# Linear attention on one Trainium2 core: when the first octet's output is stored

## The chip, the core and the metric

The kernel runs on one core of one Trainium2 chip. The metric is the device time of one execution in microseconds (us), as the median of several runs. The engines are named as in the profile: PE (TensorE; PEld is its weight load), DVE (VectorE), ACT (ScalarE), POOL (GpSimd, which here only issues the loads) and SP (SyncE, which issues the stores).

## The reference

Linear attention with a ReLU feature map, for 8 batches, 12 heads, 512 positions and 64 features, all in f32:

```python
Q_feat = np.maximum(0, Q)
K_feat = np.maximum(0, K)
KV = np.einsum('bhkd,bhkv->bhdv', K_feat, V)
K_sum = np.sum(K_feat, axis=2)
numerator = np.einsum('bhqd,bhdv->bhqv', Q_feat, KV)
denominator = np.einsum('bhqd,bhd->bhq', Q_feat, K_sum)
return (numerator / (denominator[:, :, :, None] + 1e-10)).astype(np.float32)
```

## The kernel before

The 96 heads (batch times head) are taken in 12 *octets* of eight. K and V are loaded in 24 groups of four heads, two groups to an octet, as tiles of 128 partitions by 16 rows of 64 features; Q in one tile of 128 by 32 rows for each octet. The loads turn f32 into bf16 on the way (all but the first K and V group, which SP loads as f32). Each K or V load writes 256 KB and reads 512 KB, each Q load writes 512 KB and reads 1 MB. One octet's output is 1 MB of f32.

**Loads.** All loads but the first two are issued by POOL, in the order of the code: for each octet K, V, K, V, Q (`load_k` L93, `load_v` L97, `load_q` L101). There are 12 buffers each for K and V tiles and 7 for Q tiles.

**The work of one octet.** `prep` (L139, L141) and `prep_v` (L146 on ACT, L148 on DVE) apply the ReLU to K and spread K and V over head-wise masked copies; `mm_kv` (L153) multiplies them on PE and `evac_kv` (L163) copies the result to SBUF. `qt` transposes Q on PE (`transp`, L174) and ACT applies the ReLU (`relu_q`, L182). `denom` (L224 on PE, L227, L232 and L236 on DVE) makes the reciprocals of the denominators. `out_t` (L204 on PE, L206 on ACT) makes the transposed numerators. `backs` transposes them back in two halves (`back`, L242), normalises each half on DVE (`norm`, L248) and calls `store`. The order of the work is written out by hand: in the loop over octets, the transposes back, the normalisation and the store of octet o - 1 stand behind the K-V products of octet o; in the last octets this is shifted (`SAME`). The last octet is written out by itself and its store goes in two halves (L261).

**Stores.** `store` issues on SP. `DELAY` is 5, and there are 7 output buffers of 1 MB; the f32 tile of the first K and V group uses one of them at the start. Ahead of an octet's store, SP issues a tiny DMA (L256) of 64 bf16 numbers from the K tile of group 2(o + 5) to a scratch tile nobody reads. It can only be issued when that K load has landed, and since SP issues in order, the store (L263) behind it waits for the load too. The first seven octets, 0 to 6, have such a K tile (groups 10, 12, ... 22); from octet 7 on, the store waits only for its own normalisation. Each tiny DMA also writes the scratch tile that the one before wrote, so it waits for that one to land.

Of the kernel before, what the change touches and what calls it, by code (L numbers as in the profile page):

```python
# [10 lines left out]
def kernel(  # L11
# [20 lines left out]
    NO = NG // 2  # L32
    assert NO * 8 == NH and R == 16 and RQ == 32
    DELAY = 5
# [217 lines left out]


    def store(o, o_sb):
        if o + DELAY < NO:
            nc.sync.dma_start(out=scratch, in_=k_sb[2 * (o + DELAY)][0:1, 0, :])  # L256
        Ov = Or[o].rearrange("p (r d) -> p r d", d=D)
        if o == NO - 1:
            for j in range(2):
                rs = slice(RQ // 2 * j, RQ // 2 * (j + 1))  # L260
                nc.sync.dma_start(out=Ov[:, rs], in_=o_sb[:, rs])  # L261
            return
        nc.sync.dma_start(out=Ov, in_=o_sb)  # L263
# [22 lines left out]
    def backs(o):  # L286
        o_sb = out_tile()
        for j in range(2):
            norm(o, j, back(o, j), o_sb)
        store(o, o_sb)  # L290
# [26 lines left out]
    o = NO - 2  # L317
# [15 lines left out]
    for i in range(2):  # L333
        relu_q(o + 1, i, transp(o + 1, i), nc.vector if i == 1 else None)
    norm(o, 1, ps, o_sb)
    store(o, o_sb)
    idle(5, o + 1)
    out_u(o + 1, 0)
# [32 lines left out]
```

## Time and profile before

| what | value |
|---|---|
| median of 3 runs | 126.78 us (126.53 to 127.32) |
| the profiled execution: its time | 127.21 us |
| the profiled execution: its span, first to last instruction | 125.4 us |
| busy: PE, DVE, ACT, POOL | 69%, 64%, 63%, 26% of the span |
| loads issued by POOL: share of the 16 DMA engines | 77.1% |
| stores, tiny DMAs and first loads issued by SP: share of the 16 DMA engines | 27.0% |
| traffic at the DRAM over the span | 401 GB/s |
| first octet's normalisation (L248) | 23.20 to 25.56 us |
| first tiny DMA and first store issued | 42.14 and 42.77 us |
| last store's first half issued | 118.76 us |

All times within the execution are counted from the span's start. Lines such as L248 are lines of the kernel printed above. In a row of a timeline the first two numbers are the start and the duration, then come the engine (SPq is SP's queue of DMA issues), the line, the operation, out<-in, and in brackets how long the engine sat idle before it and what ended that. In the view by windows the columns are the stretch and its length, busy time and number of instructions on PE, PEld, DVE, ACT and POOL, the granted PE clock as a share of full speed, the DMA share and the GB/s moved, as bytes written. In the rows of DMA queues, q0 holds POOL's loads and q1 what SP issues: packets, megabytes and share of the 16 engines.

### The profile page before, as it was taken

The page shows a single profiled execution, that of the slowest core. Times are in us where ns is not written, and L with a number is a line of the kernel's source. Part 1 is how long each engine was busy: PE and PEld are TensorE (multiplying, and loading weights), DVE is VectorE, ACT ScalarE, POOL GpSimd, SP SyncE. Part 2 cuts the span into 40 slices and gives each one's busy share as a digit, 9 for nine tenths or more (in the row PEclk, how much of TensorE's full clock was granted, in tenths as well). Part 3 has the DMA queues.
Part 4 walks back from the last instruction along what each step waited for, and adds up shares of the span by engine and source line. Part 5 has one row for each costly group of instructions (what it writes and reads, how often), then busy time and mean ns, then how long its engine had stood idle before and what let it go on. Part 6 is the DMA issues. An engine that isn't in the chain of part 4 may idle for free.

```text
span 125.4 us, 2673 instructions
## 1 busy us (share of the span) xinstructions
PE 86.5 (69%) x1075; PEld 78.7 (63%) x1075; DVE 80.3 (64%) x176; ACT 79.5 (63%) x114; POOL 32.9 (26%) x64
## 2 busy tenths in 40 slices
PE   0056779979598992891698596199867767797700
PEld 0055669879397881880697494199766566696600
DVE  2686175697968979289047839632946937989620
ACT  0383895898979977686329787364929828637300
POOL 6953324333162431241133115034031000000000
PEclk9999986999999999998559999657999999999997
DMA  4999999999999999999999999999999999999992
GB/s 148 299 218 201 214 206 211 213 211 215 206 214 206 210 189 323 246 218 310 269 215 282 301 212 262 323 208 240 339 220 216 334 247 214 325 427 421 426 412 103
DMA packets 10748, 32.15 MB, mean 256 GB/s; under 512 B 1392, under 2 KB 1392, under 8 KB 9328
## 3 DMA queue, kind: packets, MB, share of 16 engines
q0 software_dynamic: 8352, 18.35, 77.1%
q1 hardware_dynamic: 2384, 13.63, 27.0%
q8 instruction: 8, 0.13, 0.4%
q14 instruction: 4, 0.03, 0.1%
HBM read 37.75 MB, written 12.58 MB: 401 GB/s over the span
## 4 chain that ended last, share of the span: by engine, by line
DMA 61%; DVE 15%; PE 14%; issue 2%; POOL 1%; DVEq 1%; ACT 0%; POOLq 0%
DMA v_sb<-in_V_dram 37%; DMA q_sb<-in_Q_dram 24%; DVE o_sb L248 8%; PE ps_kv L153 6%; PE ps_bk L242 4%; PE ps_qt L174 3%; DVE kf L139 2%; DVE vo L141 1%; POOL k_sb L93 1%; DVE vo L148 1%; DVEq L366 1%; DVE den L232 1%; DVE rec L236 1%; DVE qt L180 1%; DVE own L227 1%
## 5 line engine op out<-in xcount | busy, mean ns | idle before, releaser
L153 PE MATMUL ps_kv<-vo,kf 128*128 128x132 bf16 x384 | 31.3, 248 | 13.3 <-ACT vo L146 7.8
L248 DVE TENSOR_TENSOR o_sb<-ps_bk,rec 128x1024 f32<-128x1024 f32 x24 | 28.3, 1219 | 16.9 <-PE ps_bk L242 16.9
L153 PEld LDWEIGHTS <-kf 128*128 128x128 bf16 x384 | 29.1, 112 | 14.3 <-DVE vo L141 6.9
L163 ACT CAST kvd<-ps_kv 64x260 bf16<-64x260 f32 (+1 forms) x54 | 18.7, 346 | 19.4 <-PE ps_kv L153 18.2
L182 ACT ACTIVATE qt<-ps_qt 128x1024 bf16<-128x1024 bf16 x23 | 22.4, 1022 | 9.2 <-PE ps_qt L174 9.1
L139 DVE TENSOR_SCALAR kf<-k_sb,mask 128x1024 bf16<-128x1024 bf16 x46 | 19.2, 459 | 10.0 <-DMA k_sb<-in_K_dram 10.0
L206 ACT COPY ot_sb<-ps_ot 128x1024 f32<-128x1024 f32 x22 | 21.9, 1014 | 2.4 <-PE ps_ot L204 1.6
L174 PE MATMUL ps_qt<-ident,q_sb 128*128 128x128 bf16 x192 | 16.0, 250 | 10.6 <-DMA q_sb<-in_Q_dram 10.6
L242 PE MATMUL ps_bk<-ident,ot_sb 128*128 128x128 f32 x192 | 23.0, 273 | 0.0
L93 POOL DMA_DIRECT2D k_sb<-in_K_dram x23 | 12.7, 554 | 35.0 <-DMA q_sb<-in_Q_dram 22.3
L174 PEld LDWEIGHTS <-q_sb 128*128 128x128 bf16 x192 | 13.9, 114 | 12.5 <-DMA q_sb<-in_Q_dram 12.5
L242 PEld LDWEIGHTS ps_bk<-ident,ot_sb 128*128 128x128 f32 x192 | 20.9, 141 | 0.0
L97 POOL DMA_DIRECT2D v_sb<-in_V_dram x23 | 13.1, 570 | 19.8 <-DMA k_sb<-in_K_dram 10.5
L204 PE MATMUL ps_ot<-qt,kvd 128*128 128x256 bf16 x88 | 12.7, 271 | 4.5 <-DVE o_sb L248 4.5
L141 DVE TENSOR_SCALAR vo<-v_sb,mask 128x1024 bf16<-128x1024 bf16 x23 | 11.2, 485 | 3.1 <-DMA v_sb<-in_V_dram 3.1
L146 ACT ACTIVATE vo<-v_sb,mask 128x1024 bf16<-128x1024 bf16 x11 | 12.7, 1152 | 0.3
L204 PEld LDWEIGHTS <-kvd 128*128 128x128 bf16 x88 | 8.2, 97 | 6.7 <-issue 6.0
L224 PEld LDWEIGHTS <-qt 128*128 128x128 bf16 x192 | 6.7, 96 | 4.7 <-ACT qt L182 3.4
L224 PE MATMUL ps_den<-kvd,qt 128*128 128x16 bf16 x192 | 7.5, 179 | 2.7 <-ACT qt L182 2.1
L101 POOL DMA_DIRECT2D q_sb<-in_Q_dram x12 | 6.5, 541 | 7.3 <-DMA v_sb<-in_V_dram 5.8
L227 DVE SCALAR_TENSOR_TENSOR own<-ps_den,mask_h 128x256 f32<-128x256 f32 x12 | 5.0, 416 | 3.1 <-PE ps_den L224 3.1
L148 DVE TENSOR_SCALAR vo<-v_sb,mask 128x1024 bf16<-128x1024 bf16 x12 | 5.8, 480 | 0.0
(27 smaller groups left out, 26.2 us busy)
## 6 DMA issues: line engine op xcount, KB each, us to landing
out_dram<-o_sb SPq DMA_DIRECT2D x11, 1024.0 KB, 9.1
q_sb<-in_Q_dram POOLq DMA_DIRECT2D x12, 512.0 KB, 14.8
k_sb<-in_K_dram POOLq DMA_DIRECT2D x23, 256.0 KB, 13.7
v_sb<-in_V_dram POOLq DMA_DIRECT2D x23, 256.0 KB, 13.2
out_dram<-o_sb SPq DMA_DIRECT2D x2, 512.0 KB, 4.4
kv_first<-in_K_dram SPq DMA_DIRECT2D x1, 512.0 KB, 3.2
kv_first<-in_V_dram SPq DMA_DIRECT2D x1, 512.0 KB, 4.0
scratch<-k_sb SPq DMA_DIRECT2D x7, 0.1 KB, 4.8
```

Of the source, the lines that this page charges most:

```text
L93: nc.gpsimd.dma_start(out=k_sb[g].rearrange("p r d -> p (r d)"), in_=Kr[g], single_packet=True)
L97: nc.gpsimd.dma_start(out=v_sb[g].rearrange("p r d -> p (r d)"), in_=Vr[g], single_packet=True)
L139: nc.vector.tensor_scalar(kf[g][:, :, s, :], k_sb[g], scalar1=0.0, scalar2=mask[:, 0, s:s + 1], op0=Alu.max, op1=Alu.mult)
L153: nc.tensor.matmul(ps_kv[:, g % 2, 0:2 * (D + 2)].rearrange("p (t d) -> p t d", t=2), kf[g][:, r, :, :].rearrange("p s d -> p (s d)"), vo[ ...
L163: copy(kvd[o % NK][64 * c:64 * c + 64, 4 * gs.start + s:4 * gs.stop:2, c * D1:c * D1 + D1].rearrange("p (g t) d -> p g t d", t=2), ps_kv[6 ...
L174: nc.tensor.transpose(ps[:, u, :], q_sb[o][:, i * (U // 2) + u, :], ident)
L182: nc.scalar.activation(to, ps, Act.Relu)
L204: nc.tensor.matmul(ps[:, i], kvd[o % NK][:, h, 1:2 * D + 1], q[:, :, h, :], start=True, stop=True, skip_group_check=True)
L206: nc.scalar.copy(ot[o][:, :, 4 * j:4 * j + 4], ps.rearrange("p h u c -> p u h c"))
L224: nc.tensor.matmul(ps[:, u], qt_sb[o % NZ][:, u, :], kvd[o % NK][:, :, 0:2 * D1:2 * D1 - 1], start=True, stop=True, skip_group_check=True)
L242: nc.tensor.transpose(ps[:, 2 * v:2 * v + 2].rearrange("p c d -> p (c d)"), ot[o][:, 8 * j + v].rearrange("p h c -> p (h c)"), ident32)
L248: nc.vector.tensor_tensor(o_sb[:, rs], ps, rec[o][:, rs].unsqueeze(2).to_broadcast([P, 16, D]), op=Alu.mult)
```

## The change

The condition ahead of the tiny DMA gets a lower bound. Octet 0's store is then issued without a tiny DMA ahead of it, when octet 0 has been normalised. Octets 1 to 6 keep theirs, with the same K groups (12 to 22); octets 7 to 11 had none and have none. No other line differs.

```diff
     def store(o, o_sb):
-        if o + DELAY < NO:
+        if 0 < o < NO - DELAY:
             nc.sync.dma_start(out=scratch, in_=k_sb[2 * (o + DELAY)][0:1, 0, :])
         Ov = Or[o].rearrange("p (r d) -> p r d", d=D)
```

## The prediction

> **What bounds the kernel now.** I read the page's slices first, then the timelines of SP, POOL, PE and DVE, the chain of waits, and windows of time at the end. The slices of DMA share and of moved bytes come first:
>
> ```profile
> DMA  4999999999999999999999999999999999999992
> GB/s 148 299 218 201 214 206 211 213 211 215 206 214 206 210 189 323 246 218 310 269 215 282 301 212 262 323 208 240 339 220 216 334 247 214 325 427 421 426 412 103
> HBM read 37.75 MB, written 12.58 MB: 401 GB/s over the span
> ```
>
> The reader is to see that the transfers never rest. Up to slice 14 the rate is about 211 GB/s, but loads turn f32 in DRAM into bf16 on chip, so 211 written means 422 read. At the end, where only stores run, it is 421 to 427. Both kinds therefore run at the same traffic of some 420 GB/s at the DRAM. 50.33 MB between 2.0 and 123.2 us is 415 GB/s, so the whole kernel is within 2% of those two rates.
>
> Next, the SP queue, which issues the stores, in order of time:
>
> ```profile
> 42.14 0.59 SPq L256 DMA_DIRECT2D scratch<-k_sb  x1
> 42.77 0.57 SPq L263 DMA_DIRECT2D out_dram<-o_sb  x1
> 52.63 0.51 SPq L256 DMA_DIRECT2D scratch<-k_sb  x1
> 53.19 0.58 SPq L263 DMA_DIRECT2D out_dram<-o_sb  x1
> ...
> 103.38 0.50 SPq L256 DMA_DIRECT2D scratch<-k_sb  x1
> 103.97 11.65 SPq L263 DMA_DIRECT2D out_dram<-o_sb  x5
> 118.76 1.46 SPq L261 DMA_DIRECT2D out_dram<-o_sb  x2
> ```
>
> Each tiny copy waits until its K load has landed and the store follows at once. So these starts are also landing times: K load 10 at 42.14, 12 at 52.63, 22 at 103.38. From 12 to 22 that is five octets in 50.75 us, 10.15 each, with one store in each. Without a store, the transposes' waits put Q's tile 2 at about 26.2 (POOL's release at 26.18) and tile 4 at 40.92: 7.37 us an octet. One store of 1.05 MB thus costs the loads 2.5 us (bytes over 420 GB/s) to 2.8 us (10.15 less 7.37).
>
> The chain of waits then says who follows whom late in the kernel:
>
> ```profile
> 64.80 16.10 DMA q_sb<-in_Q_dram
> 80.89 0.05 issue
> 80.94 1.89 PE ps_qt L174 x16
> ...
> 118.74 1.13 DVEq L366
> ```
>
> Up to 80.89 the chain is loads; behind Q's tile 8 it is PE and DVE work only, 38 us of it. And the transfers at the end, by windows of two microseconds:
>
> ```profile
> 118.00:120.00 2.00, 0.34 (x4) 0.11 (x1) 1.87 (x2) 0.00 (x0) 0.00 (x0) 1.00 1.02 432
> 120.00:122.00 2.00, 0.00 (x0) 0.00 (x0) 0.00 (x0) 0.00 (x0) 0.00 (x0) 1.00 0.98 406
> ```
>
> The last two columns are DMA share and GB/s. The transfers are still full while the last store is issued, so the end is bound by bytes and by the last octet's work together.
>
> **The change part by part.** Everything is compared with this execution: span 125.4, its time 127.21, so 1.81 lies around the span; the median of the runs, 126.78, is 0.43 under that time.
>
> Removed: one tiny copy (0.59 us of SP's issue, 0.1 KB) and the wait ahead of it. The wait was 40.5 us, but nothing but stores is queued on SP and no octet waits for a store (buffer 0 of the outputs comes round again at octet 7, whose normalisation is at about 87). It also drops the wait of the second copy for the first one to land (4.7 us, over at 47.7, five before 52.63). Worth: 0, hidden under the wait for K load 12; without that cover 0.6 us.
>
> Moved: the first store, one DMA of 1 MB with 0.57 us of issue. It goes from 42.77 to the end of the first octet's normalisation:
>
> ```profile
> 23.20 2.36 DVE L248 TENSOR_TENSOR o_sb<-ps_bk,rec 128x1024 f32<-128x1024 f32 x2 [2.40 <-PE ps_bk L242]
> ```
>
> so 23.20 + 2.36 = 25.56. SP is idle there; on SP it passes no other transfer. On the engines it passes the loads on POOL's queue that are outstanding then and up to 42: the rest of octet 3's, octet 4's, and octet 5's first. How soon is it served? For store 0 as it was, issued at 42.77, the SP queue's packets in a window tell it:
>
> ```profile
> q0 software_dynamic: 225, 0.43, 113.5%
> ...
> q1 hardware_dynamic: 62, 0.42, 51.6%
> q0 software_dynamic: 52, 0.15, 43.9%
> ```
>
> The first line is 42.8 to 44.8, where q1 has no line at all; the others are 46.8 to 48.8, where the store takes half of the engines' time. So a store is served 4 us late and then over some 5 us. Moved, it is served from about 30 to 35.
>
> Cost there: loads that land after about 31 are 2.5 to 2.8 us later, I take 2.5. Q's tile 3 moves from 34.1 to about 36.5, tile 4 from 40.9 to 43.4, K load 10 from 42.1 to 44.6. Gain later: between K loads 10 and 12 there is no store now, so that stretch is 7.4 to 8 us, not 10.49, and K load 12 lands at 44.6 + 7.5 = 52.1 against 52.63. The two cancel, since the same bytes lie ahead of K load 12 in both orders. I bound the remainder: 10.49 is 0.34 over the later mean of 10.15, which could be a cost of starting the mixture and might be saved or moved; so -0.5 to +0.3, and I take -0.1.
>
> What does the lateness do to the compute? One octet takes PE 6.88 us when loads are there (first transpose of octet 5 at 50.49 to the last output product at 57.37). Octet 2's work on PE ends at 33.3 and now waits to 36.5 rather than 34.13. From 36.5 it needs till 43.4, where tile 4 arrives; then till 50.3, and tile 5 arrives at 50.5 to 51. Before, PE sat 2.39 us idle ahead of tile 5: that idle time is the cover and pays for the delay. From octet 6 on the waits for Q tiles (3.19 at 60.56, 1.09 at 70.87, 2.56 at 80.94) and all transfers are as they were.
>
> One thing on PE can go worse. The wait ahead of tile 3 grows to about 3.2 us, and in this execution a wait of 3.19 us ahead of octet 6 went with a granted clock of 0.50 from 60 to 64; that octet took 60.56 to 69.78, 9.22 us, 2.34 more than octet 5. Paid in octet 3, PE would be at 45.7, 52.6 and 59.5 at the ends of octets 3, 4 and 5, still ahead of tile 6 at 60.56: worth 0 by these rows. The Trainium skill, in "TensorE: Matmul & The Clock Gate", Part 1, says that the half rate follows an idle window of about 3.4 us that runs freely, so that a wait's place in the window decides; the trace agrees in its stretches of 6.8 us at 0.5 from 58.9 and 79.4, and by it the loss in octet 3 is a matter of luck from run to run, 0 or 2.34 there.
>
> Sum: 0 (copy) + 2.5 (loads late early) - 2.6 (no store between K loads 10 and 12) + 0 (compute, covered) = -0.1 us. 127.21 - 0.1 = 127.1 for a like execution, and 126.78 - 0.1 = 126.7 for the median.
>
> **The rivals.**
>
> A, the early stage swallows the store (faster): if the loads before 42 have room to spare, the 2.5 us there cost nothing and the 2.5 us after K load 10 are won to the end: 126.78 - 2.5 = 124.3. For it: compute has tiles in store early (POOL issues loads some 13 us before they land). Against: the DMA row reads 9 in every slice from 26 to 42 with 211 GB/s, no room, and the end has to drain the same six stores. The Trainium skill, in "HBM Reference", Access, gives about 425 GB/s for a core streaming alone; 50.33 MB at that rate is an estimate of 118.4 us against the 121.2 between 2.0 and 123.2, so A would need nearly all of that room.
>
> B, the loads do not catch up (slower): loads are let out when the load eight before has landed (POOL's issues wait for landings all along). If after the early store this keeps the queue thin, the stretch from K load 10 to 12 stays near 10 us though no store is in it. Price: the 2.5 us, and all later loads and stores late by it: 129.3. Place and point: K load 12 landing past 54 decides for it. For it: POOL waits for a landing before most issues. Against: octets without a store already ran at 7.37 us under the same limit.
>
> C, the half rate moves to the end (slower): if octet 3 runs at half rate, octet 6 starts without a long wait and the half-rate stretch moves from octets 6 and 8 to 7 and 9 or 10, where no load wait covers it. Price 2.34 less the slack of the end: the last half store lands 4.4 us after issue, the first load of that size, with nothing ahead of it, 3.2; slack 1.2. So 1.1 and up: about 128.0. If instead octet 8 merely loses its half rate, the end stays with the transfers, -0.3.
>
> D, it doesn't do what it says: store 0 could still be held by another semaphore on SP. Nothing in its waits shows one; time 126.8.
>
> **How the numbers follow.** The forecast with D has 0.66, its own range 126.1 to 127.5. A has 0.12, B 0.12, C 0.10. A comparison of this kernel tells about 1% (1.27 us) from no change: A is faster; B and the dearer part of C slower, 0.20 with C's cheaper part within 1%; so faster 0.12, same 0.68, slower 0.20. The range 125.8 to 128.8 leaves out A and part of B. Predicted time 126.7.
>
> **What would show it.** Right: the SP timeline has a store at about 25.6 and six tiny copies, the first at 52 to 53; written rates above 250 GB/s near 30 to 35 and none from 43 to 52; PE's wait ahead of tile 3 about 2.4 us longer, that ahead of tile 5 gone or short; the starts at 63, 73, 83, 93 and 103 within 0.6 us of before; DMA share full to about 123. Wrong: K load 12 before 51 (A) or past 54 (B), a PE clock of 0.5 after 91 with DMA share falling before the last store (C), a first store near 42 (D).

## The result, and the profile after

The changed kernel takes 127.64 us in the median of 20 runs (127.45 to 127.77) against 126.80 of the kernel before in 20 runs (126.47 to 127.32). The ratio is 1.0064, 95% interval 1.0052 to 1.0075: slower by 0.84 us. The time lies in the stated range (125.8 to 128.8), above the forecast's own (126.1 to 127.5); the forecast change of -0.1 us was wrong. In a few executions (one of six of a2, one of six of prime_1, four of six of free) the granted clock was lower and the time 1.4 to 12% longer; every ratio here leaves them out.

The profiled execution took 127.64 us with a span of 125.8. Its SP queue in order of time (start, duration, line, out<-in, count):

```profile
24.33 0.35 SPq L263 DMA_DIRECT2D out_dram<-o_sb  x1
53.66 0.59 SPq L256 DMA_DIRECT2D scratch<-k_sb  x1
54.29 0.57 SPq L263 DMA_DIRECT2D out_dram<-o_sb  x1
...
103.74 0.50 SPq L256 DMA_DIRECT2D scratch<-k_sb  x1
104.34 12.10 SPq L263 DMA_DIRECT2D out_dram<-o_sb  x5
119.57 1.46 SPq L261 DMA_DIRECT2D out_dram<-o_sb  x2
```

The store goes at 24.33, and there are six tiny copies. K load 12 lands at 53.66, not at 52.1 as forecast and later than the 52.63 of before. The page's slices of DMA share and bytes:

```profile
DMA  4999999999999999999999999999999999999992
GB/s 130 300 217 205 214 206 216 210 161 329 247 206 212 211 208 222 199 217 289 293 210 271 318 207 238 344 214 225 340 233 214 318 262 214 321 421 427 417 417 115
```

The share is full throughout, as before. But slice 8, where the store has been issued, shows 161 GB/s where loads alone make about 211. The 329 of the next slice do not make up for it, since they hold the store's bytes. By windows of two microseconds (the last two columns are DMA share and GB/s):

```profile
24.00:26.00 2.00, 0.60 (x4) 0.29 (x3) 1.93 (x6) 1.88 (x2) 0.53 (x1) 0.95 1.07 206
26.00:28.00 2.00, 1.66 (x16) 1.67 (x17) 1.44 (x5) 0.53 (x2) 0.74 (x2) 0.50 1.13 155
28.00:30.00 2.00, 2.00 (x27) 2.00 (x25) 0.41 (x2) 1.41 (x2) 0.53 (x1) 0.70 1.00 265
```

The engines count as busy (1.13, 1.00) while they move less: the packets themselves take longer. The loads' queue from 26 to 28 us, in the changed kernel and then in the kernel before (packets, MB, share of the engines):

```profile
q0 software_dynamic: 172, 0.31, 112.9%
```

```profile
q0 software_dynamic: 228, 0.42, 112.3%
```

For the same share of the engines there are 172 packets instead of 228, and none of the store's yet. From here on this is called *the dip*. The kernel before has a smaller one, at 46 to 48, ahead of its own first store:

```profile
44.00:46.00 2.00, 1.93 (x20) 1.76 (x18) 1.12 (x2) 1.33 (x4) 0.86 (x2) 1.00 1.19 214
46.00:48.00 2.00, 1.52 (x24) 1.10 (x23) 1.97 (x4) 1.95 (x3) 0.53 (x1) 1.00 0.99 203
48.00:50.00 2.00, 0.10 (x1) 0.00 (x0) 1.97 (x6) 1.29 (x2) 0.00 (x0) 1.00 1.01 342
```

Here 203 stands for less traffic than 203 of loads alone would, since the store's bytes, which count once and not twice, are already among them.

**A measure for the dip.** The DMA queues of the stretch 24 to 52 us hold it in every kernel with one store in this stretch. Traffic is twice q0 (loads read f32 and write bf16) plus q1. The changed kernel, then a second profile of the kernel before, then k12 of experiment 2, whose first store comes so late (50.59) that its packets lie behind 52:

```profile
q0 software_dynamic: 2342, 5.13, 98.9%
q1 hardware_dynamic: 144, 1.05, 9.2%
```

```profile
q0 software_dynamic: 2402, 5.24, 99.2%
q1 hardware_dynamic: 176, 1.05, 9.4%
```

```profile
q0 software_dynamic: 2740, 5.85, 109.8%
```

That is 11.31, 11.53 and 11.70 MB. 11.70 MB in 28 us, 0.418 MB a us, is the rate at which these kernels run where there is no dip, and no kernel shows more from 24 to 52. (From 56 to 104 us the kernel before moves 2 x 7.38 + 5.24 = 20.00 MB, 0.417 a us.) What is missing from 11.70 is called the loss; 1 MB is 2.39 us.

### The profile page after: what moved, and what is told of

Same layout as the page of the kernel before. It is cut to its first block, busy times and chain, and to the rows that moved or that the text cites. A ratio compares the mean times of both kernels' runs of the same rounds, so it can differ in the third digit from the quotient of the medians.

```text
span 125.8 us, 2671 instructions
## 1 busy us (share of the span) xinstructions
PE 88.5 (70%) x1075; PEld 80.7 (64%) x1075; DVE 80.7 (64%) x176; ACT 79.4 (63%) x114; POOL 33.8 (27%) x64
## 4 chain that ended last, share of the span: by engine, by line
DMA 68%; PE 14%; DVE 6%; POOL 4%; issue 2%; DVEq 1%; ACT 0%; POOLq 0%
DMA q_sb<-in_Q_dram 36%; DMA v_sb<-in_V_dram 22%; DMA k_sb<-in_K_dram 10%; PE ps_kv L153 5%; PE ps_bk L242 5%; DVE o_sb L248 4%; PE ps_qt L174 3%; POOL v_sb L97 1%; POOL k_sb L93 1%; DVEq L366 1%; POOL q_sb L101 1%; DVE kf L139 1%; DVE qt L180 1%; PE ps_den L191 1%; PE ps_ot L217 0%
## 5 line engine op out<-in xcount | busy, mean ns | idle before, releaser
L153 PE MATMUL ps_kv<-vo,kf 128*128 128x132 bf16 x384 | 31.9, 251 | 13.9 <-DVE kf L139 7.9
L242 PE MATMUL ps_bk<-ident,ot_sb 128*128 128x128 f32 x192 | 24.2, 281 | 0.0
L93 POOL DMA_DIRECT2D k_sb<-in_K_dram x23 | 13.2, 572 | 34.4 <-DMA q_sb<-in_Q_dram 16.0
L242 PEld LDWEIGHTS ps_bk<-ident,ot_sb 128*128 128x128 f32 x192 | 22.2, 148 | 0.0
L97 POOL DMA_DIRECT2D v_sb<-in_V_dram x23 | 13.6, 589 | 20.2 <-DMA k_sb<-in_K_dram 9.5
```

The lines of the kernel that those rows point to most:

```text
L93: nc.gpsimd.dma_start(out=k_sb[g].rearrange("p r d -> p (r d)"), in_=Kr[g], single_packet=True)
L97: nc.gpsimd.dma_start(out=v_sb[g].rearrange("p r d -> p (r d)"), in_=Vr[g], single_packet=True)
L153: nc.tensor.matmul(ps_kv[:, g % 2, 0:2 * (D + 2)].rearrange("p (t d) -> p t d", t=2), kf[g][:, r, :, :].rearrange("p s d -> p (s d)"), vo[ ...
L242: nc.tensor.transpose(ps[:, 2 * v:2 * v + 2].rearrange("p c d -> p (c d)"), ot[o][:, 8 * j + v].rearrange("p h c -> p (h c)"), ident32)
```

## The experiments

All kernels but those named otherwise differ from the kernel before in one place; diffs of kernels that start from the changed one say so. Each ratio is to the kernel before on the same chip.

**1. Both kernels once more: a2 (the changed one) and b2 (the one before), no edit.**

> The changed kernel once more, for a second profile and a second ratio. In the first pair of profiles the changed one lay 0.16 MB of traffic (0.38 us) behind already at 16 us, before anything differs, and another 0.11 MB behind after its first store. Theory S (a loss at the first store): in every execution the loads' traffic falls below 300 GB/s for about two microseconds just before the first store's first packets, and this loses more when that store is early (0.90 us against 0.64). It expects the ratio again near 1.006, the dip again at 27 to 29, and no lag at 16 us against the kernel before's second profile. Rival T (a later half-rate stretch of PE in the last octets): expects PE's clock at 0.5 somewhere after 100 us again, and the last store issued 0.8 us late with the transfers no later than before.

> The kernel before once more: ratio 1.000. Its first profile was an execution of 127.21 us, 0.41 over its median; both theories expect a profile with a span near 125.0. It tells how much of the differences between the two profiles is chance: K load 12 landing at 52.63 give or take 0.4.

Measured: a2 1.0068 (1.0049 to 1.0087), loss 0.45 MB; b2 0.9992 (0.9978 to 1.0006), loss 0.17 MB, K load 12 at 52.76. The first two profiles lay apart before anything differs, which was chance: by the queues up to 24 us the changed kernel had moved 9.11 MB and the one before 9.23, but a2 and b2 9.13 each. (At 16 us they were 0.06 MB apart, not the expectation's 0.16.) In the first pair this 0.12 MB and the 0.06 MB by which the losses differ make 0.43 us, and the two executions are 127.64 - 127.21 = 0.43 us apart. The half-rate stretch that the changed kernel's profile had at 107 to 111 is chance as well, and costs nothing. The last store of a2:

```profile
118.62 1.46 SPq L261 DMA_DIRECT2D out_dram<-o_sb  x2
```

It is issued 0.95 us earlier than in the first profile (119.57), yet the span is 125.9 against 125.8. Here the end follows the bytes, not the compute, and theory T falls: a2 is as slow without the half-rate stretch.

**2. When the first store goes: k8, k12, and the control k1.**

```diff
         if o + DELAY < NO:
-            nc.sync.dma_start(out=scratch, in_=k_sb[2 * (o + DELAY)][0:1, 0, :])
+            late = 8 if o == 0 else 2 * (o + DELAY)      # k12: 12, k1: 1
+            nc.sync.dma_start(out=scratch, in_=k_sb[late][0:1, 0, :])
```

> Store 0 waits for K load 8 in place of K load 10, so it goes at about 35.5 in place of 42.8; all else as in the kernel before. Theory S: the loss lies between those of 25 and 43 if it depends on how early the store is: 1.002 to 1.005. Theory T (the tail): no relation to the store's time, 0.998 to 1.007. Theory U (a store is harmful only where compute has not got ahead of the loads, before about 30): 1.000.

> Store 0 waits for K load 12 in place of 10, so stores 0 and 1 go one behind the other at about 50. Theory F with a cost that falls with time (1.0 us at 25, 0.75 at 35, 0 to 0.6 at 43): 0.996 to 1.000. If a store must be somewhere before K load 12 for the end to come out (the bytes at the end): 1.002 or more.

> The kernel before, with store 0's tiny copy taken from K load 1, which landed before 8 us, in place of K load 10: the same instructions as the kernel before, with the first tiny copy early (at about 1 to 24 us, as SP gets to it) and the store at about 25. Theory S: the time is that of the early store, 1.004 to 1.008. Rival V (the copy that was taken away absorbed part of the loss, by waking the queue): 1.000 to 1.002.

Measured: k8, with the store at 35.58, 1.0042 (1.0024 to 1.0060), loss 0.31. k12, store at 50.59, 0.9980 (0.9964 to 0.9997), loss 0, the only version whose interval lies below 1, by a hair. The stretch up to 52 ends before a dip of k12 could come, so its queues from 52 to 62, where its first store and most of the second run, have to be read too:

```profile
q0 software_dynamic: 510, 1.18, 61.3%
q1 hardware_dynamic: 301, 1.81, 45.5%
```

That is 4.17 MB in 10 us, 0.417 a us: no dip there either. k1, which keeps every instruction of the kernel before, with its first tiny copy at 6.65 and the store at 24.66, 1.0064 (1.0045 to 1.0084), loss 0.47. So it is the store's time and not the copy that was taken away (theory V falls), and from 25 us on the cost falls with the time: 0.39 to 0.49 at 25 (the table below, without act and half), 0.31 at 36, 0.05 to 0.33 at 43, 0 at 51. The ratios fall in the same order: 1.0064, 1.0042, 1 and 0.9980. Theory U (no harm from 30 on) falls with k8.

**3. An early small write to spare the big store: prime_b, prime_a, prime_1, and prime_s within SBUF.** The edit, into the kernel before (prime_b) or the changed one (the others):

```diff
         zero(g)
+        if g == 0:
+            nc.sync.dma_start(out=Or[NO - 1][:, 0:4], in_=mask.rearrange("p a b -> p (a b)"))
         prep(g)
```

prime_1 writes `[0:1, 0:4]` only, prime_s writes to an SBUF tile.

> The kernel before with one more DMA: at about 2 us SP writes 4 numbers of each partition from the mask tile to the place of the last octet's output, which the real store writes over much later. Theory S1 (the dip belongs to the first write to the output at all): the dip before the first big store is gone, 0.6 us saved there, ratio about 0.995. Theory S2 (the dip belongs to the first big store, or to the change from loads alone to a mixture): the dip stays at 45 to 48 and the ratio is 1.000 to 1.003.

> The changed kernel with one more DMA: at about 2 us SP writes 4 numbers of each partition to the place of the last octet's output (the real store writes over them later). Theory S1 (the loss of 0.9 to 1.1 us before the first big store belongs to the first write to DRAM and is dearer when it comes early): the dip at 27 to 29 is gone, the lag behind the kernel before at 52 us shrinks from 0.2 MB to nothing, and the ratio is 0.998 to 1.002 in place of 1.0066. Theory S2 (the loss belongs to a big store beside loads this early, or to the copy that was taken away): dip and ratio stay, 1.005 to 1.009.

> Control for the run beside it: the changed kernel with the same early DMA of 4 numbers of each of the 128 partitions, but within SBUF, to a tile that nobody reads. S1 with DRAM as the place: dip and ratio stay as in the changed kernel, 1.005 to 1.009. If an early DMA on SP's queue of any kind is what does it, the ratio falls to 0.998 to 1.002 as well.

> The changed kernel with the early write to the last octet's output cut to one partition, 16 bytes, on one DMA engine of the 16. If the loss is paid once for the output as such: the dip is gone, 0.998 to 1.002. If it is paid by each engine or for each region written: the dip stays, 1.005 to 1.008, or falls only a little.

Measured: prime_b 1.0002 (0.9980 to 1.0023), loss 0.05 in its profile. That profile would have spoken for S1, but the ratio does not (S1 expected 0.995), and the dip is not spared in the others: prime_a 1.0081 (1.0060 to 1.0101), loss 0.43; prime_s 1.0072 (1.0054 to 1.0090), loss 0.49; prime_1 1.0068 (1.0049 to 1.0088; only its times are used). An early small write spares nothing. With the store at 43 the loss changes from execution to execution, and prime_b's profile was one with little.

**4. How often and for what it is paid: two_early, tiny25, half.**

```diff
-        if o + DELAY < NO:
+        if 1 < o < NO - DELAY:                                    # two_early
...
+        if o == 0:                                                # tiny25, ahead of the tiny copy
+            nc.sync.dma_start(out=Ov[:, 0, 0:4], in_=o_sb[:, 0, 0:4])
...
+        if o == 0:                                                # half, ahead of the tiny copy
+            nc.sync.dma_start(out=Ov[:, 0:RQ // 2], in_=o_sb[:, 0:RQ // 2])
```

Dots stand between edits of different kernels. In half, the other half of store 0 goes in the old place, behind the tiny copy.

> Stores 0 and 1 both without a tiny copy ahead (stores 2 to 6 keep theirs), so store 1 goes at about 32. Seen so far: each kernel with store 0 at 25 loses 0.36 to 0.43 MB of traffic (0.9 to 1.0 us) in the two microseconds before that store's first packets, whether a tiny copy or a small early write comes before it or not; with store 0 at 43 it loses 0 to 0.25 MB. Theory F (only the first big store pays): 1.006 to 1.008, the same as the change. Theory E (every store in the stage of loads alone pays 0.9 us): 1.012 to 1.015. Theory L (the loads' lateness counts, not the dip): 1.010 or more, K load 14 later than 64.5.

> The kernel before with one more small DMA: when octet 0 is normalised, SP stores 4 numbers of each partition of it (16 bytes times 128); the whole 1 MB store follows behind K load 10 as before. If the loss is a matter of starting a write in the stage of loads at all, there is a dip at 27 to 29 and the ratio is 1.003 to 1.007. If it needs the 1 MB, no dip at 27 to 29 and 1.000 to 1.002.

> Store 0 in two halves: 512 KB when octet 0 is normalised, 512 KB behind K load 10. If the early start is paid once whatever its size: a dip of 0.36 to 0.43 MB at 27 to 29 and a ratio near 1.007. If it goes with the bytes: half of it, 1.003. If each half pays: 1.008 or more.

Measured: two_early 1.0062 (1.0043 to 1.0080), traffic 11.26 with two stores in the stretch, loss 0.44: the second early store pays nothing. The windows ahead of its bytes and with them:

```profile
34.00:36.00 2.00, 0.00 (x0) 0.00 (x0) 1.21 (x4) 0.25 (x1) 0.67 (x2) 1.00 1.04 211
36.00:38.00 2.00, 0.00 (x0) 0.00 (x0) 0.10 (x1) 0.00 (x0) 0.22 (x1) 0.72 1.09 361
```

tiny25 0.9998 (0.9981 to 1.0014), no dip at 27. half 1.0067 (1.0044 to 1.0090), loss 0.56 in its profile, a dip at 24 to 27 and a thin stretch at 32 to 33 (162 GB/s, the engines at 0.81), none before its second half. So it is paid once, by the first big store, and half a store is big.

**5. Whose first store, and how big: early_big, act, ramp, quarter, warm64.** early_big, act and warm64 start from the changed kernel. ramp and quarter, from the kernel before, store the first rows early and the rest behind K load 10; warm64 stores both pieces early.

```diff
+    nc.sync.dma_start(out=Or[NO - 1][:, 0:R * D], in_=k_sb[0].rearrange("p r d -> p (r d)"))   # early_big
...
+        if o == 0:                                   # act
+            nc.scalar.dma_start(out=Ov, in_=o_sb)
+            return
...
+        if o == 0:                                   # ramp, warm64; quarter: 0:8
+            nc.sync.dma_start(out=Ov[:, 0:2], in_=o_sb[:, 0:2])
```

> The changed kernel with one more 512 KB store: as soon as the first K group's f32 tile has landed (about 4 us), SP writes it to the first half of the last octet's output, which the real store writes over at the end. The extra bytes alone cost 0.52 MB over 0.42 MB a us, 1.25 us. If the first big store as such pays, whenever: a dip at about 5 to 8, none at 25 to 29, ratio near 1.0066 + 0.0099 = 1.0165 or less, should the dip be cheaper there. If the state of the loads at 25 is what pays (SP's store meeting a long run of loads alone): the dip stays at 25 to 29 as well, 1.0165 to 1.025.

> The changed kernel with store 0 issued by ACT in place of SP, at the same place in the order of the work (ACT waits for the normalisation, some 0.5 us, and spends about 0.5 us on the issue). If the loss belongs to the first big store of a queue: a dip at 27 to 29 for ACT's store and another at the first store of SP behind K load 12; ratio 1.006 to 1.010. If it belongs to SP's queue only: no dip at 27 to 29, 0.998 to 1.003. If to the first big store of the core: one dip, 1.006 to 1.008.

> The kernel before, with the first 512 bytes of each partition of octet 0's output (64 KB) stored at about 25, the rest behind K load 10. If any store with more than a few packets pays once: a dip at 27 to 29 of some 0.4 MB, none at 45 to 48, ratio 1.004 to 1.007. If the dip needs long packets or hundreds of KB: no dip at 27 to 29, ratio 0.999 to 1.002.

> The kernel before, with the first 2 KB of each partition of octet 0's output (256 KB) stored at about 25, the rest behind K load 10. If the payment grows with the bytes of the early piece (0 at 64 KB, 0.36 to 0.45 MB at 512 KB): a dip of about 0.15 to 0.25 MB at 27 to 29, ratio 1.002 to 1.005. If it is all or nothing from some size on: a dip of 0.36 MB or more and 1.005 to 1.008, or none and 0.999 to 1.001.

> The changed kernel with store 0 in two pieces one right behind the other, both at about 25: 64 KB, then the other 960 KB. If a small piece ahead spares the big one: no dip at 27 to 30, ratio 0.997 to 1.002. If the big piece pays whatever runs ahead of it: a dip of 0.36 to 0.45 MB and 1.006 to 1.008.

early_big is the clearest run. Its windows:

```profile
5.00:6.00 1.00, 0.00 (x0) 0.00 (x0) 1.00 (x2) 0.70 (x1) 1.00 (x2) 1.00 1.14 176
6.00:7.00 1.00, 0.00 (x0) 0.10 (x1) 0.53 (x5) 0.99 (x2) 0.73 (x2) 1.00 1.07 164
7.00:8.00 1.00, 0.21 (x3) 0.20 (x3) 0.73 (x2) 0.74 (x1) 0.74 (x1) 1.00 1.16 176
...
27.00:28.00 1.00, 0.72 (x11) 0.47 (x7) 1.00 (x2) 0.95 (x2) 0.00 (x0) 1.00 1.14 211
28.00:29.00 1.00, 0.75 (x10) 0.70 (x10) 0.95 (x3) 0.88 (x2) 0.39 (x1) 1.00 1.10 207
29.00:30.00 1.00, 1.00 (x22) 1.00 (x20) 0.98 (x4) 1.00 (x2) 0.31 (x2) 1.00 1.13 211
```

With a 512 KB store at 4 us, the dip is at 5 to 9, and the octet's store, which here goes at 28.23, finds none: loss 0.01 MB from 24 to 52. The big store at 4 us went to another octet's place in the output, so it is not the place that is paid for. The ratio, 1.0150 (1.0128 to 1.0173), is the extra bytes (0.0099) and about one payment: 0.0051 is left, and the change costs 0.0064, within that interval. act 1.0081 (1.0062 to 1.0099), a dip at 25 to 28: ACT's queue pays as well, and SP's first store at 54.66 pays nothing after it; but a first store that late was free in k12 too, so whether each queue would pay is not told apart. ramp 0.9997 (0.9979 to 1.0015): 64 KB early cost nothing. quarter 1.0012 (0.9989 to 1.0036): 256 KB cost little in the median; its profiled execution was its slowest (127.80 us, loss 0.34), with the fall at 32 to 34, behind the early piece and not ahead of it. Its times spread from 126.58 to 127.80, so whether 256 KB pay in some executions stays open. warm64 1.0054 (1.0036 to 1.0072), loss 0.41: a small piece ahead does not spare the big one.

**6. No waits at all: free.**

```diff
-        if o + DELAY < NO:
+        if o < 0:
```

> No tiny copies: every store goes as soon as its octet is normalised. Theory F (one payment, then bytes are bytes): K and Q tiles come one store later for each octet from 25 on, but the end is set by the same bytes; ratio 1.005 to 1.009. Rival (stores ahead of the loads starve the compute, and the last octets come out late): 1.015 or more, with DMA share falling at the end.

Measured: 1.0482 (1.0447 to 1.0516), from two executions. One dip, and up to 116 us as much traffic as a2. Then, by windows:

```profile
116.00:118.00 2.00, 1.99 (x26) 1.76 (x24) 1.93 (x4) 0.49 (x2) 0.00 (x0) 1.00 1.02 393
118.00:120.00 2.00, 1.07 (x18) 1.07 (x19) 0.58 (x2) 0.89 (x3) 0.00 (x0) 1.00 0.30 123
120.00:122.00 2.00, 1.65 (x31) 1.34 (x30) 1.97 (x3) 1.25 (x2) 0.00 (x0) 1.00 0.00 0
```

The transfers run dry, because every load came later by the stores ahead of it and Q's last tile is there only at about 118.9. Here the rival holds: the compute behind the last load is the end, and theory F was wrong in that. The waits together are worth 6 us, but the first of them only what the change cost.

**All profiles together.** Loss from 24 to 52 us, and the time of that same execution:

| kernel | first big store at, us | loss, MB | time, us |
|---|---|---|---|
| k12 | 50.6 | 0.00 | 126.46 |
| prime_b | 43.1 | 0.05 | 126.51 |
| tiny25 | 42.9 | 0.11 | 126.72 |
| ramp | 43.4 | 0.15 | 126.80 |
| before, second profile | 43.1 | 0.17 | 126.94 |
| k8 | 35.6 | 0.31 | 127.25 |
| before, first profile | 42.8 | 0.33 | 127.21 |
| changed kernel | 24.3 | 0.39 | 127.64 |
| warm64 | 25.0 | 0.41 | 127.45 |
| prime_a | 26.0 | 0.43 | 128.19 |
| two_early | 25.1 | 0.44 | 127.68 |
| changed kernel, second profile | 25.2 | 0.45 | 127.74 |
| k1 | 24.7 | 0.47 | 127.62 |
| prime_s | 25.5 | 0.49 | 127.82 |
| act | about 24 | 0.53 | 127.89 |
| half (512 KB) | 23.1 | 0.56 | 128.60 |

From k12 to k1 the time rises by 1.16 us for 0.47 MB, 2.47 us a MB; bytes over the rate make 2.39. The others lie within 0.25 us of the line through k12 with 2.39 us a MB, and within 0.17 us if the bytes are counted from 0 us on, which takes in what was lost or won before the store. (The table's times come from several chips, on which the kernel before has medians of 126.68 to 126.88.) Three executions lie 0.5 to 0.8 us above the line, prime_a, half and quarter (0.34 MB, 127.80 us), each the slowest of its kernel's. What sets them apart comes after 120 us. In quarter the last octet came late and the transfers ran dry (238 GB/s at 120 to 121). half's last bytes drained late, 98 GB/s from 124 to 125 and 12 after that, where a2 moved 45 and none; why, and what held prime_a, is not shown. It also fits that the kernel before spreads over 0.85 us in its runs, with losses of 0.17 and 0.33 in its two profiles, and the changed one only over 0.32, with 0.39 and 0.45.

## Why the prediction was wrong

- The picture of the bound held: full transfers from start to end, 0.42 MB a us, and an end that follows the bytes.
- The moves came as described. Store 0 went at 24.33 and not 25.56, since octet 1 did not start at half rate this time (its transposes of Q took 1.07 us, not 1.84). Q's tile 3 was taken up at 37.34 (forecast 36.5), with PE at half rate behind it, and PE's wait ahead of tile 5 was gone. PE's transposes of Q in the changed kernel:

```profile
37.34 1.89 PE L174 MATMUL ps_qt<-ident,q_sb 128*128 128x128 bf16 x16 [2.79 <-DMA q_sb<-in_Q_dram]
46.62 1.06 PE L174 MATMUL ps_qt<-ident,q_sb 128*128 128x128 bf16 x16
53.72 1.06 PE L174 MATMUL ps_qt<-ident,q_sb 128*128 128x128 bf16 x16
61.50 1.07 PE L174 MATMUL ps_qt<-ident,q_sb 128*128 128x128 bf16 x16 [0.52 <-DMA q_sb<-in_Q_dram]
```

  The cover sufficed: at 61.50 PE waits for a load again. The half rate of octet 3 lasted from 36.0 to 42.9 and cost nothing at the end. Its length is two of the free-running windows of about 3.4 us that the Trainium skill gives in "TensorE: Matmul & The Clock Gate", Part 1. The window ahead of it was not wholly idle, though: PE was busy for 1.42 of the 3.4 us up to 36.0. The later starts were to stay within 0.6 us of before and did not quite: 63.73, 73.94, 83.72, 93.70 and 103.74 are 0.36 to 0.97 later.
- **The step that failed is the cancelling of +2.5 and -2.6.** It took the bytes ahead of K load 12 as all that counts, and put the remainder at -0.1, bounded by -0.5 and +0.3; the time moved by +0.84. K load 12 came at 53.66 and 53.86 in the two profiles of the changed kernel, against 52.63 and 52.76. The bytes cancel; what does not is the payment at the first big store, 0.39 to 0.49 MB at 25 against 0.05 to 0.33 at 43. Between the means of the profiles in the table with the store at 25 (0.44, seven of them without act and half) and at 43 (0.16, five) that is 0.28 MB, 0.67 of the 0.84 us; the rest is not accounted for by these few profiles. The prediction had this term in hand, as the 0.34 us by which the stretch from K load 10 to 12 is longer than later ones, and took it as a thing to be saved or moved at its size. Both halves of that were wrong. In the very execution that it was read from, the loss was 0.33 MB, 0.79 us. And it is not of fixed size: in the means it nearly triples when the store goes at 25.
- A smaller reading does not hold either. PE's row at 40.92 shows no wait for a load, so it is no landing time of Q's tile 4, and the 7.37 us an octet read from it are only near: an octet's loads are 3.15 MB of traffic, 7.5 us at 0.418 MB a us. The sum went by 2.5 and 7.5, so this changes nothing in it.
- Rival A: refuted, no room in the early stage. (The figure of about 425 GB/s that was weighed there stands in the Trainium skill, "HBM Reference", under Specifications (TRN2), not Access; the runs here reach 418.) B: the right sign and place, K load 12 late, but by 1.1 us and not past 54, and not for the reason given: the loads from 40 to 52 ran at 195 to 229 GB/s in the windows, 211 on average, their full rate. C: half-rate stretches did move in the first profile (octet 7 and 107 to 111 us), and a2, which has none after 100 us before its last store and is no faster, shows that the late one cost nothing. D: refuted by the SP timeline.

**What stays open** is why the first big store costs the loads' packets time, and why less the later it comes. Shown are the size of the cost, that it is paid once, that it takes more than 64 KB, that ACT's queue pays as SP's does, and that neither a small write nor a 64 KB piece ahead of it spares it. That the fall lies right ahead of the store's first packets is true of most profiles, but not of quarter's.

## What to carry to other kernels

Where transfers are full from end to end and stay so, moving a transfer changes the time only by what the move does to the rate (free shows what happens where they do not stay so); count therefore the bytes moved in fixed stretches of both profiles before explaining anything by waits or clocks. A dip of one or two microseconds in the moved bytes at full DMA share is a cost that no chain of waits names. Of the places tried here the first big store is best issued behind K load 12, by 0.2%, and the other waits are what keeps the last loads, and with them the last octets, early.

## What the runs showed of the hardware

- The first store of 512 KB or more beside a full stream of loads cost 0.39 to 0.56 MB of traffic (0.9 to 1.3 us) at about 25 us, 0.31 MB at 36, 0.05 to 0.33 MB at 43, and nothing at 51; a second one, whose bytes moved from 36 on, cost nothing (two_early). Meanwhile the loads' packets took longer: from 26 to 28 us 172 of them filled the share of the engines that 228 fill in the kernel before.
- A store issued into full queues moved its first bytes only some 4 us later: it was issued at 24.33, the window 26 to 28 still holds loads alone, at 155 GB/s, and from 28 on the store's bytes raise the rate to 265.
- The clock of PE hardly mattered to the time: the changed kernel's 20 runs had mean granted clocks from 0.898 to 0.945, and those at 0.898 took 127.45, 127.62 and 127.64 us, the one at 0.945 127.62.
